# Layer 1 attention: where the gate product, the one-column scale steps and the near blocks' units are computed

## The chip, the cores and the metric

The kernel runs on one core of a Trainium2 chip. Its engines are TensorE (PE in the profile, with its weight loads as PEld), VectorE (DVE), ScalarE (ACT) and GpSimd (POOL); SyncE (SP) issues the DMAs. Each engine works through a list of its own in order and waits on semaphores for the others. The metric is the device time of one execution in microseconds, as the median of the runs.

## The reference

Two decoder layers and a final norm, on 1024 positions of width 1024 with 16 heads of 64. Layer 0 is attention with a forget gate; layer 1, to which this change belongs, is attention with three branches per head: over compressed blocks, over chosen blocks, and over a window of the last 512 positions. Its core, cut:

```python
lg = jnp.einsum('btgrd,btgnld->btgrnl', qc, kb).astype(jnp.float32) * scale   # chosen blocks
p = jax.nn.softmax(jnp.where(m, lg, NEG).reshape(...), axis=-1)
...
lg_w = jnp.einsum('bnqgrd,bnkgd->bngrqk', qb, k_band).astype(jnp.float32) * scale   # window
p_w = jax.nn.softmax(jnp.where(m_w[None, :, None, None], lg_w, NEG), axis=-1)
...
g = jax.nn.sigmoid(gate_raw).reshape(B, S, G, R, N_BRANCH)
o = g[..., 0:1] * o_c + g[..., 1:2] * o_s + g[..., 2:3] * o_w
return (o.reshape(B, S, W) * jax.nn.silu(z)) @ w_out
```

## The kernel before, in words

The program runs layer 0, then the projections and the compressed branch of layer 1, then the stage this change is about, and last the output projection with the final norm. In that stage `NsaSuper(h, s)` stands for one head `h` and one half `s` of the positions (512 queries), and the 32 of them run in order, `s` = 1 ahead of `s` = 0 in each head.

Each has eight units, `unit(y, qi)`: `qi` counts four tiles of 128 queries, `y` = 0 is the chosen blocks (128 to 1024 keys), `y` = 1 the window, here called the near blocks (128 to 640 keys). A unit goes from engine to engine. PE makes the scores `S` in PSUM (L1662). One custom DVE instruction (L1670) multiplies the scores by a scalar, adds a mask, writes the result to `P` in SBUF and keeps the minimum of each row; a second instruction of the same line reads that minimum out into `m`. For `y` = 0 the scalar of L1670 is a column of per-partition values (`units`), for `y` = 1 it is the constant 1.0, and the units come in afterwards: L1672 multiplies `m` by `units` and adds a constant. ACT then takes the exponential in place (L1673), with `m` as its bias and, for `y` = 1, a column of `units` as its scale, and sums each row into `l`. For `y` = 1 POOL splits the result into two halves of lower precision (L1676 the high part, L1677 the rest, into a ring of three `hl` buffers), and an SP transpose brings them to `hT`. For `y` = 0 PE transposes into `ptp` (L1695), ACT and DVE split that into `pth` and `ptl` (L286, L287). PE multiplies both with the values into `O` (L1703 to L1705).

`finish()` closes a group of eight units: DVE takes the reciprocals of the eight row sums per partition (L1735), multiplies them by the gates (L1736), and later multiplies `O` by the product (L1738, into `u`); POOL adds the two branches (L1739).

Between these units the list is filled with work of the layer's `z` projection (`nz`, L269 to L271). For each of its eight column blocks `nz_scale(p)` computes a scale on one column per partition in seven short DVE steps (L1475, two in `half_root` at L222 and L224, L1477 to L1481); `z_scale(p)` at L597 does likewise in layer 0. `zq`, in the profile `nzq`, is the small tile of these columns.

The order on each engine is set ahead of time: `run_attn` interleaves the units of the next group with the steps of this one, `merge` mixes in the filler by the costs that the generators yield, and a scheduler then places the instructions by its own account of when each could run.

Of the kernel before, what the change touches and what calls it, by code (L numbers as in the profile page):

```python
# [13 lines left out]
AF = mybir.ActivationFunctionType  # L14
OP = mybir.AluOpType
# [18 lines left out]
LNUP = 15 * 0.6931471805599453  # L34
# [7 lines left out]
def tile_fox_nsa(ctx, tc, a, out):  # L42
    nc = tc.nc
    V, A, G, T = nc.vector, nc.scalar, nc.gpsimd, nc.tensor
# [12 lines left out]
    def ps_s2(name):  # L57
        return psS.tile([P, 2, 512], F32, tag="S", name=name)
# [22 lines left out]
    ready = {}  # L81
# [6 lines left out]
    class Norm:  # L88
# [11 lines left out]
        def finish(self, g, parts=1, eng=None):  # L100
            st, h, x = self.st, self.h, self.x
            if self.n == 2:
                V.tensor_tensor(st[:, 0:1], st[:, 0:1], st[:, 1:2], OP.add)
            A.activation(st[:, 2:3], st[:, 0:1], AF.Sqrt, bias=eps, scale=1.0 / D)
            V.reciprocal(st[:, 3:4], st[:, 2:3])
            for i in range(parts):
                c = slice(i * D // parts, (i + 1) * D // parts)
                if eng is None:
                    V.scalar_tensor_tensor(h[:, c], x[:, c], st[:, 3:4], g[:, c], OP.mult, OP.mult)
                else:  # L110
                    eng.tensor_scalar(h[:, c], x[:, c], st[:, 3:4], 1.0, OP.mult, OP.mult)
                    eng.tensor_tensor(h[:, c], h[:, c], g[:, c], OP.mult)
            return h
# [105 lines left out]
    def half_root(q, c):  # L219


        V.tensor_scalar(q[:, c + 1:c + 2].bitcast(I32), q[:, c:c + 1].bitcast(I32), 24, 23,  # L222
                        OP.logical_shift_right, OP.logical_shift_left)
        V.tensor_scalar(q[:, c + 2:c + 3].bitcast(I32), q[:, c + 1:c + 2].bitcast(I32), 0x3F800000, None, OP.bitwise_xor)  # L224

    late_on = tc.keep_in_program_order
# [366 lines left out]
    def z_scale(p):  # L593


        zq = ready["zt", p]["q"]
        late_on(V.tensor_tensor(zq[:, 2:3], zq[:, 0:1], zq[:, 1:2], OP.add))  # L597
        half_root(zq, 2)
        V.tensor_scalar(zq[:, 5:6], zq[:, 4:5], 2.0 ** 46, None, OP.mult)
        V.scalar_tensor_tensor(ao[0][:, p:p + 1], zq[:, 3:4], 2.0 ** 81, ready["v", p][1], OP.mult, OP.mult)  # L600
        ready["c", p] = zq[:, 5:6]
# [387 lines left out]
    gates = pers.tile([P, NT, 48], F32, name="gates")  # L989
# [481 lines left out]
    def nz_scale(p):  # L1471


        zq = ready["zt", p]["q"]
        late_on(V.tensor_tensor(zq[:, 2:3], zq[:, 0:1], zq[:, 1:2], OP.add))  # L1475
        half_root(zq, 2)
        V.tensor_scalar(zq[:, 5:6], zq[:, 4:5], 2.0 ** 74, None, OP.mult)  # L1477
        V.tensor_tensor(zq[:, 6:7], zq[:, 5:6], ready["limits"][:, p // 2:p // 2 + 1], OP.mult)
        V.tensor_scalar(zq[:, 6:7], zq[:, 6:7], 2.0 ** 100, None, OP.min)
        V.tensor_scalar(zq[:, 7:8].bitcast(I32), zq[:, 6:7].bitcast(I32), 0x7F800000, None, OP.bitwise_xor)  # L1480
        V.tensor_scalar(ao1[:, p:p + 1], zq[:, 7:8], 0.5, None, OP.mult)  # L1481
        ready["c", p] = zq[:, 6:7]
# [120 lines left out]
    bias = []  # L1603
# [4 lines left out]
    class NsaSuper:  # L1608
# [30 lines left out]
        def unit(self, y, qi):  # L1639
            h, s, g = self.h, self.s, self.g  # L1640
            if self.first:
                self.pre()
                self.first = False
            k = KV[g, y][0]
            i = 4 * s + qi
            nm = f"{self.name}_{y}_{qi}"
            k0 = P * max(0, i - 4) if y else 0
            n = P * (i + 1) - k0
            ps = ps_s2(f"S_{nm}")
            if y:  # L1650
                L = at.tile([P, 640], F32, tag="Pw", bufs=5, name=f"P_{nm}")[:, 0:n]
            else:
                L = at.tile([P, n], F32, tag=f"P{s}{qi}", bufs=1, name=f"P_{nm}")
            m = at.tile([P, 1], F32, tag="m", bufs=8, name=f"m_{nm}")
            mk = bias[qi] if s and not y else wmask[:, 640 - n:]
            w = n if n <= 512 else n // 2
            if (h, s, y, qi) == (H - 1, 0, 1, 3):
                ready["scores"] = True
            c = 0
            for b in range(n // w):  # L1660
                for x in range(2):
                    T.matmul(ps[:, b, 0:w], self.q[x][:, qi * P:(qi + 1) * P], k[:, k0 + b * w:k0 + b * w + w],  # L1662
                             start=(x == 0), stop=(x == 1))
                c += 2 * max(107, w * 0.42)
            if w == n:
                src, dst, mk = ps[:, 0, 0:n], L, mk
            else:
                src, dst, mk = ps[:, :, 0:w], *(x.rearrange("p (a k) -> p a k", a=2) for x in (L, mk))
            unit, minus = ready["units"][0:2]
            V.tensor_tensor_reduce(dst, src, mk, 1.0 if y else unit, 3e38, OP.add, OP.min, m)  # L1670
            if y:
                V.tensor_scalar(m, m, unit, LNUP, OP.mult, OP.add)  # L1672
            A.activation(L, L, AF.Exp, bias=m, scale=minus if y else -1.0, accum_out=self.l[:, y, qi:qi + 1])  # L1673
            if y:
                hl = at.tile([P, 1280], F16, tag="hl", bufs=3, name=f"hl_{nm}")
                G.tensor_copy(hl[:, 0:n], L)  # L1676
                G.tensor_tensor(hl[:, n:2 * n], L, hl[:, 0:n], OP.subtract)  # L1677
                b = 2 * n // P
                nc.sync.dma_start_transpose(self.hT[:, self.at:self.at + b, :], hl[:, 0:2 * n])
                self.Ps[y, qi] = self.at, k0  # L1680
                self.at += b
            else:
                self.Ps[y, qi] = L, k0
            yield c
# [45 lines left out]
        def finish(self):  # L1730
            h, s, l = self.h, self.s, self.l
            p, j = h // 2, h % 2
            if j == 0:
                self.O[p, s, "t"] = at.tile([P, 4, P], F32, tag="ot", bufs=2, name=f"ot_{self.name}")
            V.reciprocal(l, l)  # L1735
            V.tensor_tensor(l, l, gates[:, 4 * s:4 * s + 4, 3 * h + 1:3 * h + 3].rearrange("p q y -> p y q"), OP.mult)  # L1736
            u = at.tile([P, 4, 2, 64], F32, tag="u", bufs=1, name=f"u_{self.name}")
            V.tensor_tensor(u, self.po, l.rearrange("p y q -> p q y")[:, :, :, None].to_broadcast([P, 4, 2, 64]), OP.mult)  # L1738
            G.tensor_tensor(self.O[p, s, "t"][:, :, 64 * j:64 * j + 64], u[:, :, 0], u[:, :, 1], OP.add)  # L1739
            if j and s == 0:  # L1740
                ready["done", p] = True
# [163 lines left out]
```

## Time and profile before

| | |
|---|---|
| median of 3 runs | 1460.36 us (1455.6 to 1462.95) |
| profiled execution | 1458.12 us, its span 1456.2 us |
| busy over the span | PE 94%, PEld 64%, DVE 77%, ACT 63%, POOL 40% |
| stage of the change | about 960 to 1385 us of the span |

A row of the grouped view names the line, engine, operation, tiles and shape, then the count; behind the bar stand the busy microseconds and the mean nanoseconds of one, then the idle time of that engine just before them and what ended it. The chain of waits is followed back from the last instruction: at each step to what released it, or to the instruction ahead of it on its engine. PE's busy time includes the tails of pipelined matmuls.

### The profile page before, as it was taken

Reading aid. Unit: us, or ns where it says so; the run is one execution under the profiler, and the core shown is the slowest. Engines: PE = TensorE matmul, PEld = TensorE weight load, DVE = VectorE, ACT = ScalarE, POOL = GpSimd, SP = SyncE. Lnnn points to the kernel's source line nnn. Section 1 sums busy time; section 2 is a strip of 40 time slices with the busy share of each in tenths; the row PEclk is TensorE's granted clock in tenths of the full one; section 3 lists DMA queues with packets and bytes.
Section 4 is the critical chain, followed back from the end, with each engine's and each line's share of the span. In section 5 each row is a group of like instructions: output and inputs, shape, how many; then the busy total and the mean of one; then the engine's idle time right before and its main releaser. Section 6 shows DMA issues by size and latency. Waiting matters only on the chain. (4 is left out here: it accounts for less than half of the span.)

```text
span 1456.2 us, 30393 instructions
## 1 busy us (share of the span) xinstructions
PE 1368.0 (94%) x10499; PEld 928.0 (64%) x10499; DVE 1120.3 (77%) x3016; ACT 915.9 (63%) x2328; POOL 585.3 (40%) x781
## 2 busy tenths in 40 slices
PE   5999999999999989999999988889999999998998
PEld 4778888888888745445545544446666766666643
DVE  6587787787878698486757677878999899989834
ACT  5376667776767665155555475667877778778512
POOL 2142433434334251231203456245766766765500
PEclk9999999999999999999999999999999999999999
DMA  5379798898988999354654446454667676776434
GB/s 197 96 164 191 188 185 199 203 186 198 189 197 180 244 230 203 107 176 151 189 174 141 134 121 159 119 148 92 135 151 164 140 171 123 135 169 150 95 109 145
DMA packets 414922, 234.72 MB, mean 161 GB/s; under 512 B 334448, under 2 KB 372656, under 8 KB 414768
## 3 DMA queue, kind: packets, MB, share of 16 engines
q1 hardware_dynamic: 414768, 232.78, 67.1%
q8 instruction: 83, 1.36, 0.4%
q14 instruction: 71, 0.58, 0.1%
HBM read 120.31 MB, written 28.38 MB: 102 GB/s over the span
## 5 line engine op out<-in xcount | busy, mean ns | idle before, releaser
L1662 PE MATMUL S_n<-nk,nq 128*128 128x320 f16 (+5 forms) x768 | 154.6, 314 | 13.5 <-DVE m_n L1670 12.6
L785 ACT ACTIVATE P<-P,m 128x512 f32<-128x512 f32 (+1 forms) x192 | 116.3, 607 | 53.9 <-DVE m L776 52.6
L1677 POOL TENSOR_TENSOR hl_n<-P_n,hl_n 128x640 f16<-128x640 f32 (+4 forms) x128 | 144.8, 1132 | 10.0
L756 POOL TENSOR_TENSOR Bd<-B,tri 128x128 f32<-128x128 f32 x128 | 62.4, 502 | 205.8 <-DVE m L776 189.3
L787 DVE SCALAR_TENSOR_TENSOR hl<-P,hl 128x512 f16<-128x512 f32 (+1 forms) x192 | 116.0, 620 | 28.7 <-ACT hl L786 27.2
L1676 POOL CAST hl_n<-P_n 128x640 f16<-128x640 f32 (+4 forms) x128 | 76.4, 597 | 122.1 <-ACT P_n L1673 97.3
L1673 ACT ACTIVATE P_n<-P_n,m_n 128x640 f32<-128x640 f32 (+7 forms) x128 | 98.7, 771 | 30.2 <-DVE m_n L1670 29.6
L1673 ACT ACTIVATE P_n<-P_n,m_n,units 128x640 f32<-128x640 f32 (+4 forms) x128 | 100.1, 782 | 22.5 <-DVE m_n L1672 20.6
L1662 PEld LDWEIGHTS <-nq 128*128 128x128 f16 x768 | 71.4, 98 | 60.4 <-issue 25.5
L286 ACT ACTIVATE pth_n<-ptp_n 128x512 f16<-128x512 f32 (+1 forms) x160 | 85.1, 545 | 38.9 <-PE ptp_n L1695 38.3
L287 DVE SCALAR_TENSOR_TENSOR ptl_n<-ptp_n,pth_n 128x512 f16<-128x512 f32 (+1 forms) x160 | 99.6, 632 | 7.9 <-ACT pth_n L286 5.9
L1695 PE MATMUL ptp_n<-ident,P_n 128*128 128x128 f32 x576 | 93.2, 279 | 7.5 <-ACT P_n L1673 2.2
L786 ACT ACTIVATE hl<-P 128x512 f16<-128x512 f32 (+1 forms) x192 | 92.4, 512 | 1.9 <-DMA pT<-hl 0.5
L1670 DVE CUSTOM_DVE_ANT_0 P_n<-S_n,wmask 128x640 f32<-128x640 f32 (+4 forms) x128 | 83.1, 650 | 7.2 <-PE S_n L1662 6.3
L1695 PEld LDWEIGHTS ptp_n<-ident,P_n 128*128 128x128 f32 x576 | 64.9, 141 | 33.4 <-DVE ptl_n L287 7.3
L183 ACT ACTIVATE sq<-sq,zg 128x512 f32<-128x512 f32 (+2 forms) x73 | 59.5, 815 | 22.8 <-DMA sq<-in_nsa_w_dram 17.8
L1703 PE MATMUL O_n<-nv,pth_n 128*128 128x64 f16 x576 | 71.7, 193 | 1.0 <-ACT pth_n L286 0.6
L97 ACT ACTIVATE h_n<-xr 128x512 f32<-128x512 f32 x32 | 20.0, 625 | 83.6 <-DVE xr L1795 41.4
L1704 PE MATMUL O_n<-nv,pth_n 128*128 128x64 f16 x576 | 71.8, 193 | 0.0
L1670 DVE CUSTOM_DVE_ANT_0 P_n<-S_n,bias,units 128x640 f32<-128x640 f32 (+1 forms) x64 | 68.8, 1074 | 2.9 <-PE S_n L1662 2.3
L1705 PE MATMUL O_n<-nv,ptl_n 128*128 128x64 f16 x576 | 68.7, 193 | 0.9 <-DVE ptl_n L287 0.9
L767 PE MATMUL S<-KH,Q 128*128 128x512 f32 (+1 forms) x192 | 65.0, 354 | 2.6 <-DVE m L776 2.3
(514 smaller groups left out, 4731.6 us busy)
## 6 DMA issues: line engine op xcount, KB each, us to landing
sq<-in_nsa_w_dram SPq DMA_DIRECT2D x40, 256.0 KB
B<-cD SPq DMA_DIRECT2D x16, 512.0 KB
nq<-qD SPq DMA_DIRECT2D x64, 128.0 KB
x<-in_x_dram SPq DMA_DIRECT2D x8, 512.0 KB
wst_k<-in_fox_w_dram SPq DMA_DIRECT2D x8, 512.0 KB
wst_v<-in_fox_w_dram SPq DMA_DIRECT2D x8, 512.0 KB
sq<-in_fox_w_out_dram SPq DMA_DIRECT2D x16, 256.0 KB
wst_q<-in_fox_w_dram SPq DMA_DIRECT2D x8, 512.0 KB
```

Source lines behind the costliest of these rows:

```text
L286: A.activation(hi[:, 0:n], pt[:, 0:n], AF.Copy, scale=scale)
L287: V.scalar_tensor_tensor(lo[:, 0:n], pt[:, 0:n], scale, h, OP.mult, OP.subtract)
L785: A.activation(L[:, 0:n], L[:, 0:n], AF.Exp, bias=init, scale=-1.0, accum_out=self.lr[:, col + c:col + c + 1])
L786: A.activation(hi[:, cs], L[:, 0:n], AF.Copy, scale=UP)
L787: V.scalar_tensor_tensor(lo[:, cs], L[:, 0:n], UP, hi[:, cs], OP.mult, OP.subtract)
L1662: T.matmul(ps[:, b, 0:w], self.q[x][:, qi * P:(qi + 1) * P], k[:, k0 + b * w:k0 + b * w + w], start=(x == 0), stop=(x == 1))
L1670: V.tensor_tensor_reduce(dst, src, mk, 1.0 if y else unit, 3e38, OP.add, OP.min, m)
L1673: A.activation(L, L, AF.Exp, bias=m, scale=minus if y else -1.0, accum_out=self.l[:, y, qi:qi + 1])
L1676: G.tensor_copy(hl[:, 0:n], L)
L1677: G.tensor_tensor(hl[:, n:2 * n], L, hl[:, 0:n], OP.subtract)
L1695: T.transpose(pt[:, (x + i) * P:(x + i + 1) * P], L[:, kb * P - k0:(kb + 1) * P - k0], ident)
L1704: T.matmul(o, hi, v[:, 64:128], start=False, stop=False)
```

## The change

Three things are written otherwise; the formula that is computed is that of before.

1. The product of reciprocals and gates (L1736) is issued on POOL instead of DVE.
2. In the steps on single columns, an addition of two columns (L597, L1475) becomes a form with one column as a per-partition scalar operand; in `nz_scale` the product with `limits` and the limit by a constant (L1478, L1479) become one such instruction.
3. For `y` = 1 the units become the scalar of L1670, as for `y` = 0. L1672 then only adds a constant, and ACT's exponential has the constant -1.0 as its scale.

```diff
@@ -594,7 +594,7 @@ z_scale
-        late_on(V.tensor_tensor(zq[:, 2:3], zq[:, 0:1], zq[:, 1:2], OP.add))
+        late_on(V.tensor_scalar(zq[:, 2:3], zq[:, 0:1], zq[:, 1:2], None, OP.add))
@@ -1472,11 +1472,10 @@ nz_scale
-        late_on(V.tensor_tensor(zq[:, 2:3], zq[:, 0:1], zq[:, 1:2], OP.add))
+        late_on(V.tensor_scalar(zq[:, 2:3], zq[:, 0:1], zq[:, 1:2], None, OP.add))
         half_root(zq, 2)
         V.tensor_scalar(zq[:, 5:6], zq[:, 4:5], 2.0 ** 74, None, OP.mult)
-        V.tensor_tensor(zq[:, 6:7], zq[:, 5:6], ready["limits"][:, p // 2:p // 2 + 1], OP.mult)
-        V.tensor_scalar(zq[:, 6:7], zq[:, 6:7], 2.0 ** 100, None, OP.min)
+        V.tensor_scalar(zq[:, 6:7], zq[:, 5:6], ready["limits"][:, p // 2:p // 2 + 1], 2.0 ** 100, OP.mult, OP.min)
@@ -1666,11 +1665,11 @@ NsaSuper.unit
-            unit, minus = ready["units"][0:2]
-            V.tensor_tensor_reduce(dst, src, mk, 1.0 if y else unit, 3e38, OP.add, OP.min, m)
+            unit = ready["units"][0]
+            V.tensor_tensor_reduce(dst, src, mk, unit, 3e38, OP.add, OP.min, m)
             if y:
-                V.tensor_scalar(m, m, unit, LNUP, OP.mult, OP.add)
-            A.activation(L, L, AF.Exp, bias=m, scale=minus if y else -1.0, accum_out=self.l[:, y, qi:qi + 1])
+                V.tensor_scalar(m, m, LNUP, None, OP.add)
+            A.activation(L, L, AF.Exp, bias=m, scale=-1.0, accum_out=self.l[:, y, qi:qi + 1])
@@ -1733,7 +1732,7 @@ NsaSuper.finish
-            V.tensor_tensor(l, l, gates[:, 4 * s:4 * s + 4, 3 * h + 1:3 * h + 3].rearrange("p q y -> p y q"), OP.mult)
+            G.tensor_tensor(l, l, gates[:, 4 * s:4 * s + 4, 3 * h + 1:3 * h + 3].rearrange("p q y -> p y q"), OP.mult)
```

The scheduler places the instructions anew. Behind the edit at L1478 the lines of the changed kernel have a number lower by one.

On POOL, at head 7, half 1, the product comes to stand between the two halves of the split of the group's last near block (`hl`, key tile 3). Before:

```order
L1627 TENSOR_SCALAR bias_11357<-selb 128x896
L1739 TENSOR_TENSOR ot_n_0_15180<-u_n_0_15183 128x4x64
L1676 CAST hl_n_1_1_3_15146<-P_n_1_1_3_15137 128x640
L1677 TENSOR_TENSOR hl_n_1_1_3_15146<-P_n_1_1_3_15137,hl_n_1_1_3_15146 128x640
L1676 CAST hl_n_0_1_0_15234<-P_n_0_1_0_15227 128x128
```

After:

```order
L1738 TENSOR_TENSOR ot_n_0_15176<-u_n_0_15179 128x4x64
L1675 CAST hl_n_1_1_3_15142<-P_n_1_1_3_15133 128x640
L1735 TENSOR_TENSOR l_n_1_14979<-l_n_1_14979,gates 128x8
L1676 TENSOR_TENSOR hl_n_1_1_3_15142<-P_n_1_1_3_15133,hl_n_1_1_3_15142 128x640
L1675 CAST hl_n_0_1_0_15230<-P_n_0_1_0_15223 128x128
```

One row is added, and the second half of the split now stands behind it.

On DVE, at the end of head 6, half 1, with the fourth column block's scale among it (`nzq`). Before:

```order
L1735 RECIPROCAL l_n_1_14448<-l_n_1_14448 128x8
L1672 TENSOR_SCALAR m_n_0_1_1_14753<-m_n_0_1_1_14753,units 128x1
L1475 TENSOR_TENSOR nzq_13610<-nzq_13610 128x1
L1736 TENSOR_TENSOR l_n_1_14448<-l_n_1_14448,gates 128x8
L222 TENSOR_SCALAR nzq_13610<-nzq_13610 128x1
L287 SCALAR_TENSOR_TENSOR ptl_n_1_0_14676<-ptp_n_1_0_14670,pth_n_1_0_14675 128x512
```

After:

```order
L1734 RECIPROCAL l_n_1_14445<-l_n_1_14445 128x8
L1671 TENSOR_SCALAR m_n_0_1_1_14750<-m_n_0_1_1_14750 128x1
L1475 TENSOR_SCALAR nzq_13608<-nzq_13608 128x1
L287 SCALAR_TENSOR_TENSOR ptl_n_1_0_14673<-ptp_n_1_0_14667,pth_n_1_0_14672 128x512
L287 SCALAR_TENSOR_TENSOR ptl_n_1_1_14682<-ptp_n_1_1_14676,pth_n_1_1_14681 128x512
L222 TENSOR_SCALAR nzq_13608<-nzq_13608 128x1
```

The product is gone from DVE, the addition has its new form, and the two `ptl` moved ahead of the next short step.

On PE, where head 7's first scores (`S`, half 1, chosen blocks, key tile 0) meet head 6's last products with the values (`O`). Before, two of the four score matmuls stand some 180 rows ahead of the other two:

```order
L270 MATMUL nz_1_14660<-hT_1_7605,zw_7998 128x512
L271 LDWEIGHTS zw_7998
L271 MATMUL nz_1_14660<-hT_1_7605,zw_7998 128x512
L1662 LDWEIGHTS nq_7_1_14978
L1662 MATMUL S_n_1_0_0_14985<-nk_0_13075,nq_7_1_14978 128x320
L1662 LDWEIGHTS nq_7_1_14979
```

After, all four stand together behind those products:

```order
L1704 MATMUL O_n_1_14706<-nv_1_13079,hT_n_1_14446 128x64
L270 LDWEIGHTS zw_7998
L270 MATMUL nz_1_14657<-hT_1_7605,zw_7998 128x512
L271 LDWEIGHTS zw_7998
L271 MATMUL nz_1_14657<-hT_1_7605,zw_7998 128x512
L1661 LDWEIGHTS nq_7_1_14974
L1661 MATMUL S_n_1_0_0_14981<-nk_0_13073,nq_7_1_14974 128x320
L1661 LDWEIGHTS nq_7_1_14975
L1661 MATMUL S_n_1_0_0_14981<-nk_0_13073,nq_7_1_14975 128x320
```

Heads 7, 9 and 11 had their first scores apart like this; now head 5 alone has.

## The prediction

> **What bounds the kernel now.** I first cut the span into the stage of the change and what lies around it, in the view by windows (span, then busy time of PE, PEld, DVE, ACT and POOL).
>
> ```profile
> 960.00:1385.00 425.00, 398.10 (x5011) 278.18 (x5010) 386.37 (x1053) 322.35 (x750) 266.72 (x315) 1.00 0.66 140
> 0.00:960.00 960.00, 905.64 (x5194) 620.96 (x5194) 704.87 (x1909) 578.45 (x1536) 317.45 (x465) 0.98 0.70 173
> ```
>
> In the stage DVE is busy 386.4 of 425 us (91%) and PE 398.1 (94%); ahead of it DVE has 73%. So a microsecond of DVE is worth most here, and nearly the whole change lies here. But PE has only 26.9 us free by this view. Two engines that full take turns, and the waits of the stage show it (who waited for whom: us, times, longest):
>
> ```profile
> ACT P_n L1673 <- DVE m_n L1670: 29.6, 47, 2.5
> ACT P_n L1673 <- DVE m_n L1672: 20.6, 30, 2.1
> PE S_n L1662 <- DVE m_n L1670: 12.6, 29, 1.0
> DVE P_n L1670 <- PE S_n L1662: 10.8, 26, 0.8
> DVE l_n L1735 <- ACT P_n L1673: 7.3, 13, 1.0
> PEld ptp_n L1695 <- DVE ptl_n L287: 7.3, 25, 0.9
> POOL hl_n L1676 <- ACT P_n L1673: 97.3, 53, 8.5
> ```
>
> ACT waits 50 us for DVE's minima, PE 12.6 for a score buffer that DVE holds; DVE in turn waits 10.8 for scores and 7.3 for exponentials. POOL is never the one that a long row waits for, and it stands idle 97 us ahead of the casts. Next I read the chain of waits in this stage (its shares by line, then single pieces: start, us, what):
>
> ```profile
> by line: PE S_n L1662 12.8%; DVE P_n L1670 11.6%; PE ptp_n L1695 10.1%; ACT P_n L1673 8.9%; issue 7.7%; DVE ptl_n L287 5.7%; PE O_n L1703 4.2%; PE O_n L1705 4.0%; PE O_n L1704 3.9%; PE nz L269 2.9%; PE nz L270 2.9%; PE nz L271 2.8%; ACT pth
> ...
> 991.89 0.63 DVE nzq L1475
> ...
> 999.35 0.71 DVE l_n L1736
> ...
> 1037.22 1.06 DVE l_n L1736
> ...
> 1050.69 0.83 DVE l_n L1736
> ...
> 1278.67 1.22 DVE nzq L1475
> ```
>
> ```profile
> 1350.67 0.29 DVE l_n L1736
> ```
>
> The chain changes between PE, DVE and ACT all the time: no engine alone bounds the stage. The gate product L1736 is on it in 19 pieces, from 999.35 to 1350.67, 7.1 us in all; the addition L1475 in all its 8, from 991.89 on, 4.8 us. That is a lot for products of 8 columns and sums of one. The order of time shows why (DVE, then POOL):
>
> ```profile
> 1050.69 0.83 DVE L1736 TENSOR_TENSOR l_n<-l_n,gates 128x8 f32<-128x8 f32 x1
> 1051.44 0.28 DVE L1670 CUSTOM_DVE_ANT_0 P_n<-S_n,wmask 128x128 f32<-128x128 f32 x1
> ```
>
> ```profile
> 1050.10 1.40 POOL L1677 TENSOR_TENSOR hl_n<-P_n,hl_n 128x640 f16<-128x640 f32 x1
> ```
>
> L1736 ends at 1051.52, as POOL's subtraction does (1051.50), and DVE's next minimum pass starts just then: a DVE instruction with two tensors in SBUF stands still for the rest of a POOL instruction.
>
> **The change part by part.** First what leaves DVE (by shape; busy us, mean ns):
>
> ```profile
> L1736 DVE TENSOR_TENSOR l_n<-l_n,gates 128x8 f32<-128x8 f32 x32 | 14.7, 458 | 0.7
> L1475 DVE TENSOR_TENSOR nzq<-nzq 128x1 f32<-128x1 f32 x8 | 5.4, 672 | 0.0
> L1478 DVE TENSOR_TENSOR nzq<-nzq,limits 128x1 f32<-128x1 f32 x8 | 2.6, 326 | 0.1
> L1672 DVE TENSOR_SCALAR m_n<-m_n,units 128x1 f32<-128x1 f32 x128 | 26.4, 206 | 1.3
> L1479 DVE TENSOR_SCALAR nzq<-nzq 128x1 f32<-128x1 f32 x8 | 1.1, 143 | 0.0
> ```
>
> The gate products: 32 x 458 ns = 14.7 us of DVE go, 7.1 of them on the chain. The scale steps: L1475, L1478 and L1479 take 5.4 + 2.6 + 1.1 = 9.1 us. Their two successors have a column as scalar operand, for which L1672 is the nearest row, 206 ns: 16 x 206 = 3.3, so 5.8 us of DVE go. On the chain L1475 falls from 4.8 to 8 x 0.206 = 1.6: 3.2 us.
>
> Does the new form escape POOL? The view of a line (least, median and largest ns) says so:
>
> ```profile
> L1672 DVE TENSOR_SCALAR m_n<-m_n,units x128: 192/205/215, 965.4 to 1373.4; 128x1 f32<-128x1 f32 x128
> ```
>
> ```profile
> L250 DVE TENSOR_SCALAR un<-ao,un x2: 232/717/1202, 517.5 to 1314.9; 128x8 f32<-128x8 f32 x2
> ```
>
> 128 instructions with POOL 63% busy (266.7 of 425) and none above 215 ns. With eight columns (L250) the same form took 232 once and 1202 once, so it is the single column that escapes. The Trainium skill (SBUF — State Buffer, Who interferes with whom) says that tensor_scalar too can enter a two-port mode, and that it then blocks against GpSimd like an instruction with two SBUF inputs; by that rule the new forms would stall as the old ones and the sum would lose its 3.2. For eight columns the trace agrees, for one it does not, so I take 206.
>
> The near blocks. The minimum pass gets a column as its scalar, L1672 loses it, and ACT's exponential loses one:
>
> ```profile
> L1670 DVE CUSTOM_DVE_ANT_0 P_n<-S_n,wmask,units 128x512 f32<-128x512 f32 x16 | 11.9, 741 | 0.0
> L1670 DVE CUSTOM_DVE_ANT_0 P_n<-S_n,wmask 128x512 f32<-128x512 f32 x16 | 11.0, 685 | 6.1 <-PE S_n L1662 5.6 <-POOL ot_n L1761 0.5
> ...
> L1670 DVE CUSTOM_DVE_ANT_0 P_n<-S_n,wmask,units 128x128 f32<-128x128 f32 x16 | 5.4, 338 | 0.0
> L1670 DVE CUSTOM_DVE_ANT_0 P_n<-S_n,wmask 128x128 f32<-128x128 f32 x16 | 4.5, 283 | 0.8 <-PE S_n L1662 0.5
> L1477 DVE TENSOR_SCALAR nzq<-nzq 128x1 f32<-128x1 f32 x8 | 1.2, 147 | 0.0
> L1673 ACT ACTIVATE P_n<-P_n,m_n,units 128x640 f32<-128x640 f32 x64 | 58.6, 916 | 12.3 <-DVE m_n L1672 12.0
> L1673 ACT ACTIVATE P_n<-P_n,m_n 128x640 f32<-128x640 f32 x16 | 13.3, 830 | 7.8 <-DVE m_n L1670 7.5
> ```
>
> With a column the pass takes 741 against 685 ns at 512 keys, 338 against 283 at 128: 55 to 56 ns more, 128 x 0.056 = +7.2 us. L1672 with constants alone is like L1477, 147 ns: 128 x (0.206 - 0.147) = -7.6. On DVE the two cancel, and the minimum is ready as early as before. ACT gains 916 - 830 = 86 ns each, 128 x 0.086 = 11.0 us. ACT has 103 us idle here, so only those on the chain count. L1673 is 8.9% of it, 37.8 us; all its exponentials come to 98.7 + 100.1 us on the page's two rows of L1673:
>
> ```profile
> L1673 ACT ACTIVATE P_n<-P_n,m_n 128x640 f32<-128x640 f32 (+7 forms) x128 | 98.7, 771 | 30.2 <-DVE m_n L1670 29.6
> L1673 ACT ACTIVATE P_n<-P_n,m_n,units 128x640 f32<-128x640 f32 (+4 forms) x128 | 100.1, 782 | 22.5 <-DVE m_n L1672 20.6
> ```
>
> So about 37.8 / 198.8 = 19% are on the chain, and 19% of 11.0 is 2.1 us.
>
> What POOL gets: 32 products of 8 columns. No row of POOL is that small. Nearest are the subtractions L1677:
>
> ```profile
> L1677 POOL TENSOR_TENSOR hl_n<-P_n,hl_n 128x640 f16<-128x640 f32 x64 | 92.6, 1446 | 4.8
> L1677 POOL TENSOR_TENSOR hl_n<-P_n,hl_n 128x128 f16<-128x128 f32 x16 | 6.8, 428 | 1.3
> ```
>
> A line through both (1.99 ns a column) leaves 0.19 us at 8 columns; the smallest row itself, 0.43, is the upper end. I take 0.2, the row's own slope: 6.4 us in all (13.8 at most), inside the 97.3 us that POOL idles ahead of casts. Without that cover they would delay each group's last subtraction, its transpose and the window products. `u` is in no hurry for the product (DVE):
>
> ```profile
> 1062.69 0.20 DVE L1735 RECIPROCAL l_n<-l_n 128x8 f32<-128x8 f32 x1 [1.03 <-ACT P_n L1673]
> ```
>
> ```profile
> 1075.88 0.68 DVE L1738 TENSOR_TENSOR u_n<-O_n,l_n 128x512 f32<-128x512 f32 x1
> ```
>
> The multiplication that answers to this reciprocal starts 13 us later. On POOL the product waits for the reciprocal, and behind it stands one subtraction (front part, POOL's order); the reciprocal takes 0.2 us and the cast ahead runs beside it.
>
> In layer 0 eight additions get the new form: 8 x 0.06 us by the same two rows (206 against 147), 0.5 us at most, on a DVE that is 73% busy: nothing. The moved rows on PE I price by two heads fewer whose first scores lie apart, two score matmuls and two `nz` products each, below 1 us a head: between -2 and +2, taken as nothing.
>
> **The sum.** On the chain: 7.1 + 3.2 + 2.1 = 12.4 us. That would be the gain if no other path stood close behind, but one does: PE has 26.9 us free in 425, and the reciprocal just ahead of the product had found DVE idle 13 times of 32, waiting for ACT, so DVE is not always the late one there. What is late next is PE's score and transpose matmuls, and the minimum pass that waits for them. Ends: nothing, or all DVE time that goes, 14.7 + 5.8 + 0.4 = 20.9 us. I take the chain's figure less a quarter, 9 us. The profiled execution took 1458.1 us (span 1456.2 and 1.9 around it), so its like would take 1449.1; the median shown is 2.2 above that execution, 1451.3 by it. I forecast 1450.
>
> **The rivals.** (a) DVE bounds the stage throughout: each microsecond freed is one gained. For it: the 50 us of ACT's waits for DVE, and the pieces of L1736 on the chain. Against it: DVE waits for scores 26 times. 1460.4 - 20.9 = 1439.5.
>
> (b) PE takes over: freed DVE time becomes DVE idle time ahead of L1670 and L287. For it: PE at 94%; against it: PE waits for DVE's buffers 29 times and for `ptl` 25 times, 20 us. The gain would be a third of the chain's, 4 us: 1456.
>
> (c) The column form stalls as the two-tensor form did, the rule cited above. The gain loses its 3.2 us on the chain: 1451.3 + 3.2 = 1454.5. Against it: the 128 even durations of L1672.
>
> (d) Slower: POOL becomes a link. The product waits on POOL for a reciprocal that stands in DVE's list behind other work; the subtraction behind it, its transpose and the window products come late, and PE waits at L1703. It decides once the delay eats the slack between reciprocal and `u`. With 32 groups and, as an estimate, 0.7 us each (half a subtraction of 1.4 us): 22 us, less the 9: 1473. Against it: POOL's 97 us and the 13 us above.
>
> **How the numbers follow.** My forecast, a gain of 7.5 to 14 us, has 0.40, with a range of its own of 1446 to 1453; (a) 0.15, (b) 0.25, (c) 0.08, (d) 0.10; 0.02 is left for a plain miss on the slow side. A measurement of this kernel can tell about 0.5%, 7.3 us: faster means below 1453.1. Faster: 0.40 + 0.15 = 0.55; same: 0.25 + 0.08 = 0.33; slower: 0.12. The range takes in (a) at its low end and (b) and (c) with 5 us for moved rows and spread at the other: 1439 to 1461.
>
> **What would show it.** In the changed profile: L1736 absent from DVE and 32 POOL products near 0.2 us; L1475 and the joined step even at about 0.2; passes with `units` at 640 keys near 0.87 us and the correction near 0.15; exponentials of 640 keys at 830 ns; DVE's busy time in the stage lower by about 20 us, and the stage shorter by 9. If DVE's busy time falls and the stage does not, (b) holds, and the waits of L1670 for scores will have grown. If `u` or L1703 waits for POOL or for transposes, (d). If the moved rows of PE cost more than their price, the forecast is wrong without any of these.

## The result and the profile after

| kernel | median us (lowest to highest) | ratio to the kernel before, 95% interval |
|---|---|---|
| before | 1459.2 (1451.45 to 1463.69) | 1 |
| changed | 1451.45 (1446.08 to 1456.11) | 0.9949 [0.9935, 0.9963] |
| changed, once more, beside 1459.47 | 1448.09 (1446.82 to 1454.64) | 0.9932 [0.9917, 0.9948] |

The change takes 0.51% (7.4 us) off the time in the first comparison and 0.68% (9.9 us) in the second. The forecast was 1450 with a gain of 9; of the gains that it gave as its own, 7.5 to 14 us, the first comparison just misses the lower end.

First what each piece became. The groups by shape in the stage of the changed kernel (behind the bar: busy us, mean ns of one; then the idle time before it):

```profile
L1672 ACT ACTIVATE P_n<-P_n,m_n 128x640 f32<-128x640 f32 x80 | 66.0, 825 | 14.2 <-DVE m_n L1671 11.0 <-DVE m_n L1669 2.9
...
L1669 DVE CUSTOM_DVE_ANT_0 P_n<-S_n,wmask,units 128x640 f32<-128x640 f32 x64 | 56.1, 877 | 0.2 <-PE S_n L1661 0.2
...
L1671 DVE TENSOR_SCALAR m_n<-m_n 128x1 f32<-128x1 f32 x128 | 18.8, 147 | 1.1
...
L1735 POOL TENSOR_TENSOR l_n<-l_n,gates 128x8 f32<-128x8 f32 x32 | 7.0, 219 | 0.3 <-DVE m_n L1671 0.3
...
L1478 DVE TENSOR_SCALAR nzq<-nzq,limits 128x1 f32<-128x1 f32 x8 | 1.7, 207 | 0.1
L1475 DVE TENSOR_SCALAR nzq<-nzq 128x1 f32<-128x1 f32 x8 | 1.6, 204 | 0.0
```

The single steps are at 204 and 207 ns, where their two-tensor forms took 672 and 326. The gate product takes POOL 219 ns in place of 458 on DVE. The minimum pass of 640 keys is at 877, the correction at 147, the exponential at 825.

Then the stage. Its ends are the first and the last multiplication `u`, which every group of a head ends with. The line's view, of the kernel before and of the changed one (least, median and largest ns; then first and last start):

```profile
L1738 DVE TENSOR_TENSOR u_n<-O_n,l_n x32: 634/680/692, 985.8 to 1381.4; 128x512 f32<-128x512 f32 x32
```

```profile
L1737 DVE TENSOR_TENSOR u_n<-O_n,l_n x32: 651/691/694, 988.6 to 1375.1; 128x512 f32<-128x512 f32 x32
```

From 395.6 us it came down to 386.5, by 9.1. The first `u` came 2.8 us later in this execution, so the span shrank by 6.2 only (1456.2 to 1450.0). In the second comparison's profile the stage is 386.4 long and begins at 984.9.

Third, the engines in the middle of the stage, in the view by windows (span, busy time of PE, PEld, DVE, ACT, POOL), before and changed:

```profile
1000.00:1300.00 300.00, 287.80 (x3690) 204.11 (x3690) 273.60 (x748) 232.61 (x547) 197.68 (x237) 1.00 0.68 143
```

```profile
1000.00:1300.00 300.00, 293.39 (x3766) 210.71 (x3765) 266.86 (x739) 233.04 (x567) 206.38 (x269) 1.00 0.72 148
```

In the same 300 us PE does 76 instructions more (2.1%) and is busy for 293.4 us (98%) instead of 287.8; DVE falls from 273.6 to 266.9. The waits of the changed stage say the same (who waited for whom: us, times, longest):

```profile
DVE P_n L1669 <- PE S_n L1661: 15.5, 38, 1.2
DVE l_n L1734 <- ACT P_n L1672: 8.5, 14, 0.9
...
PE S_n L1661 <- DVE m_n L1669: 8.1, 14, 1.9
...
DVE u_n L1737 <- PE O_n L1704: 5.4, 10, 1.2
...
PE O_n L1702 <- DMA hT_n<-hl_n: 1.5, 1, 1.5
...
DVE u_n L1737 <- POOL l_n L1735: 0.5, 1, 0.5
```

PE's waits for a score buffer fell from 12.6 us (29 times) to 8.1 (14 times). DVE's waits for scores rose from 10.8 (26 times) to 15.5 (38 times), and `u`, which had waited 1.6 us for the products on PE, now waits 5.4. The profile of the second comparison repeats these numbers (15.1, 37 times; 8.1, 14 times; 5.4), so they belong to the kernel and not to one execution. `u` waited for POOL once, 0.5 us.

That PE took over the stage does not follow from this. The chain of waits, by engine and as a share of the whole span, before and changed (it goes back to about 770 us in both):

```profile
PE 22%; DVE 14%; ACT 6%; issue 3%; POOL 1%; DMA 1%; SPq 0%; DVEq 0%; ACTq 0%; POOLq 0%
```

```profile
PE 20%; DVE 15%; ACT 5%; issue 3%; DMA 2%; POOL 1%; SPq 0%; DVEq 0%; ACTq 0%; POOLq 0%
```

Summed from the first `u` to the last, PE's pieces went from 189.3 us of 395.6 to 172.0 of 386.5. What came onto the chain is DMA transposes and POOL: together 3.3 us before, 18.8 in the changed kernel and 31.9 in the second comparison's profile.

### The profile page after: what moved, and what is told of

Same layout as the page of the kernel before. It is cut to its first block, busy times and chain, and to the rows that moved or that the text cites. A ratio compares the mean times of both kernels' runs of the same rounds, so it can differ in the third digit from the quotient of the medians.

```text
span 1450.0 us, 30377 instructions
## 1 busy us (share of the span) xinstructions
PE 1360.2 (94%) x10499; PEld 928.2 (64%) x10499; DVE 1105.2 (76%) x2976; ACT 906.4 (63%) x2328; POOL 590.8 (41%) x813
## 5 line engine op out<-in xcount | busy, mean ns | idle before, releaser
L1672 ACT ACTIVATE P_n<-P_n,m_n 128x640 f32<-128x640 f32 (+7 forms) x256 | 186.9, 731 | 50.1 <-DVE m_n L1669 26.9
L1669 DVE CUSTOM_DVE_ANT_0 P_n<-S_n,wmask,units 128x640 f32<-128x640 f32 (+2 forms) x192 | 124.4, 656 | 12.4 <-PE S_n L1661 11.2
L768 PE MATMUL S<-KL,Q 128*128 128x512 f32 (+1 forms) x192 | 64.7, 349 | 0.0
```

What stands on the lines that cost most here:

```text
L1669: V.tensor_tensor_reduce(dst, src, mk, unit, 3e38, OP.add, OP.min, m)
L1672: A.activation(L, L, AF.Exp, bias=m, scale=-1.0, accum_out=self.l[:, y, qi:qi + 1])
```

## The experiments

Three theories stood at the start. **A**: the pieces of the chain of waits pay, all at the rate of the whole change in the first comparison. **B**: what counts is DVE's busy time, about half of which is paid out, so the near blocks' edit, which leaves DVE's time nearly as it was, brings nothing. **C**: the gain is luck of the new order, and the parts alone bring anything. The first three runs make one part of the change each.

**The gate product alone.**

```diff
-            V.tensor_tensor(l, l, gates[:, 4 * s:4 * s + 4, 3 * h + 1:3 * h + 3].rearrange("p q y -> p y q"), OP.mult)
+            G.tensor_tensor(l, l, gates[:, 4 * s:4 * s + 4, 3 * h + 1:3 * h + 3].rearrange("p q y -> p y q"), OP.mult)
```

> The kernel before with the gate product alone on POOL. Theory A (what counts is the stall's pieces on the chain of waits, paid out at the rate of the whole change, 7.75 us of 12.4): 7.1 x 0.63 = 4.4 us faster, 1455. Theory B (DVE's own time counts, at the stage's rate of about one half): 14.7 / 2 = 7 us faster, 1452. Theory C (the gain comes from the scheduler's new order, not from the stalls): no relation to either, and the three parts alone do not add up to 7.75.

**The one-column steps alone** (the addition in `z_scale` is edited in the same way).

```diff
-        late_on(V.tensor_tensor(zq[:, 2:3], zq[:, 0:1], zq[:, 1:2], OP.add))
+        late_on(V.tensor_scalar(zq[:, 2:3], zq[:, 0:1], zq[:, 1:2], None, OP.add))
...
-        V.tensor_tensor(zq[:, 6:7], zq[:, 5:6], ready["limits"][:, p // 2:p // 2 + 1], OP.mult)
-        V.tensor_scalar(zq[:, 6:7], zq[:, 6:7], 2.0 ** 100, None, OP.min)
+        V.tensor_scalar(zq[:, 6:7], zq[:, 5:6], ready["limits"][:, p // 2:p // 2 + 1], 2.0 ** 100, OP.mult, OP.min)
```

> The kernel before with the one-column steps alone changed. Theory A: 3.2 x 0.63 = 2.0 us faster, 1457. Theory B: 5.8 / 2 = 2.9 us faster. Theory C: anything within 5 us either way.

**The units in the minimum pass alone.**

```diff
-            unit, minus = ready["units"][0:2]
-            V.tensor_tensor_reduce(dst, src, mk, 1.0 if y else unit, 3e38, OP.add, OP.min, m)
+            unit = ready["units"][0]
+            V.tensor_tensor_reduce(dst, src, mk, unit, 3e38, OP.add, OP.min, m)
             if y:
-                V.tensor_scalar(m, m, unit, LNUP, OP.mult, OP.add)
-            A.activation(L, L, AF.Exp, bias=m, scale=minus if y else -1.0, accum_out=self.l[:, y, qi:qi + 1])
+                V.tensor_scalar(m, m, LNUP, None, OP.add)
+            A.activation(L, L, AF.Exp, bias=m, scale=-1.0, accum_out=self.l[:, y, qi:qi + 1])
```

> The kernel before with the near blocks' units alone inside the minimum pass. Theory A: 2.1 x 0.63 = 1.3 us faster, 1458. Theory B: DVE's time is unchanged, so nothing, 1459. Theory C: anything within 5 us either way.

| part alone, beside 1458.63 | median us | ratio, 95% interval | gain by the ratio | piece of the chain | A | B |
|---|---|---|---|---|---|---|
| gate product | 1452.95 | 0.9961 [0.9947, 0.9976] | 5.7 | 7.1 | 4.4 | 7 |
| one-column steps | 1455.8 | 0.9976 [0.9965, 0.9988] | 3.5 | 3.2 | 2.0 | 2.9 |
| units | 1456.83 | 0.9978 [0.9964, 0.9992] | 3.2 | 2.1 | 1.3 | 0 |

All three intervals lie below 1. Each reaches some 2 us to either side, so the gate product and the steps fit A and B alike; only the units' interval (1.2 to 5.2 us) leaves out B's figure. The line of `u` in the three profiles, gate product, steps and units in turn:

```profile
L1738 DVE TENSOR_TENSOR u_n<-O_n,l_n x32: 650/688/692, 983.8 to 1375.8; 128x512 f32<-128x512 f32 x32
```

```profile
L1737 DVE TENSOR_TENSOR u_n<-O_n,l_n x32: 634/680/692, 987.5 to 1379.2; 128x512 f32<-128x512 f32 x32
```

```profile
L1738 DVE TENSOR_TENSOR u_n<-O_n,l_n x32: 677/683/693, 990.6 to 1383.3; 128x512 f32<-128x512 f32 x32
```

The stage lasts 392.0, 391.7 and 392.7 us against 395.6: 3.6, 3.9 and 2.9 less, 10.4 in all; the three edits together took 9.1. By the times the parts add up to 12.4 us, and the whole brought 7.4 and 9.9. So most of the parts' gain survives their sum. A bit is lost in all three comparisons, but with some 2 us for each part the sum of 12.4 is uncertain by 3 to 4, and beside the 9.9 the loss is not clear of that.

Is the units' 3.2 us the exponentials' doing, as A has it? The groups by shape of that kernel hold a second candidate, in instructions that it did not touch:

```profile
L1736 DVE TENSOR_TENSOR l_n<-l_n,gates 128x8 f32<-128x8 f32 x32 | 10.8, 338 | 0.7
...
L1475 DVE TENSOR_TENSOR nzq<-nzq 128x1 f32<-128x1 f32 x8 | 4.7, 591 | 0.0
L1478 DVE TENSOR_TENSOR nzq<-nzq,limits 128x1 f32<-128x1 f32 x8 | 2.0, 252 | 0.1
```

The gate products, still on DVE there, take 10.8 us instead of 14.7, and the two steps 1.3 less: in the new order they met POOL less often. So 5.2 us of DVE stalls went by placement, beside ACT's 11.0 us (915.9 to 904.9 on the pages). On this kernel's chain of waits the gate product has 10 pieces with 2.9 us, where it had 19 with 7.1. The run does not tell which of the two paid. The same holds in small for the steps' kernel, whose gate products fell to 13.2. What is saved on gate products here cannot be saved again where they leave DVE; that alone can make the parts add up to more than the whole, without any help of PE. B, which gave the units nothing, is not refuted by this gain, and C is right in so far as the order decides how long these instructions stall. That each part brings something, and the gate product most, stands.

**A column as scalar, or two tensors.** Is it the form of the instruction that escapes POOL? Two kernels add the same one-column sum to the changed one, behind the reciprocal in all 32 groups; nothing uses it. The first has two SBUF tensors, the second a column as scalar:

```diff
             V.reciprocal(l, l)
+            x = at.tile([P, 1], F32, tag="x1", bufs=3, name=f"x_{self.name}")
+            V.tensor_tensor(x, l[:, 0, 0:1], l[:, 0, 1:2], OP.add)       # first
+            V.tensor_scalar(x, l[:, 0, 0:1], l[:, 0, 1:2], None, OP.add) # second
```

> The changed kernel with 32 extra DVE sums of one column, a form with two tensors in SBUF, each behind a reciprocal of row sums; their results go nowhere. Stall theory: each stands still for the rest of a POOL instruction as the gate product did, some 400 to 500 ns, and the gate product's part of the gain is given back: 4 to 6 us slower than the change, 1455 to 1457. If an extra instruction costs its own 150 ns and no more: 1 to 2 us slower, as the next kernel.

> The same 32 extra sums in the form with one column as scalar operand. Stall theory: 206 ns each whatever POOL does, 1 to 2 us slower than the change, 1452 to 1454, and 3 to 4 us faster than the kernel with two tensors. If the count of DVE instructions is what matters and not the form: the same time as that kernel.

The two lines in their profiles:

```profile
L1736 DVE TENSOR_TENSOR x_n<-l_n x32: 148/416/981, 982.0 to 1372.7; 128x1 f32<-128x1 f32 x32
```

```profile
L1736 DVE TENSOR_SCALAR x_n<-l_n x32: 203/213/216, 980.9 to 1367.6; 128x1 f32<-128x1 f32 x32
```

The two-tensor sum takes anything from 148 ns to 981, 366 in the mean (400 to 500 were expected); the other never leaves 203 to 216. The order of time shows what ends the long ones. The longest sum of the first kernel, and what runs on POOL beside it:

```profile
1049.85 0.98 DVE L1736 TENSOR_TENSOR x_n<-l_n 128x1 f32<-128x1 f32 x1
```

```profile
1049.42 1.40 POOL L1676 TENSOR_TENSOR hl_n<-P_n,hl_n 128x640 f16<-128x640 f32 x1
```

POOL's subtraction ends at 1050.82 and the sum at 1050.83. A sum of the second kernel beside the same subtraction, in the same group:

```profile
1048.40 0.21 DVE L1736 TENSOR_SCALAR x_n<-l_n 128x1 f32<-128x1 f32 x1
```

```profile
1047.96 1.40 POOL L1676 TENSOR_TENSOR hl_n<-P_n,hl_n 128x640 f16<-128x640 f32 x1
```

This sum is done 0.75 us before POOL. Counted over all 32: in the first kernel 27 sums start while a POOL instruction runs, and 25 of these end 5 to 27 ns behind it; in the second 29 start so, and 28 of these end ahead of it. So the even durations are the form's, not the place's, and the long ones are waits for POOL. In time the two are 1454.91 (0.9978 [0.9966, 0.9991]) and 1451.89 (0.9960 [0.9947, 0.9972]) beside 1457.55: 3.0 us apart by the medians, 2.6 by the ratios, for 32 x 0.16 = 5.0 us of DVE. The intervals touch, so the size is rough. Beside the change's first ratio they are 4.2 and 1.6 us slower, within the 4 to 6 and 1 to 2 expected; beside the second, 6.7 and 4.1.

**POOL later.** If POOL were a link, more work in front of the product would cost time. This kernel adds an unused sum of 256 columns to POOL in each group:

```diff
             V.reciprocal(l, l)
+            x = at.tile([P, 256], F32, tag="x1", bufs=1, name=f"x_{self.name}")
+            G.tensor_tensor(x, l[:, 0, 0:1].to_broadcast([P, 256]), l[:, 0, 1:2].to_broadcast([P, 256]), OP.add)
             G.tensor_tensor(l, l, gates[:, 4 * s:4 * s + 4, 3 * h + 1:3 * h + 3].rearrange("p q y -> p y q"), OP.mult)
```

> The changed kernel with an extra POOL sum of 256 columns, some 0.7 us, ahead of each gate product; its result goes nowhere. It waits for the reciprocal as the product does and holds up the near blocks' last subtraction and the product. If POOL's idle time covers it: within 2 us of the change, 1450 to 1454. If POOL has become a link (rival d): 32 x 0.7 = 22 us slower, or at least 10.

```profile
L1736 POOL TENSOR_TENSOR x_n<-l_n x32: 607/611/1058, 976.3 to 1369.5; 128x256 f32<-128x256 f32 x32
```

It took 1451.03 us, 0.9954 [0.9941, 0.9968] beside 1457.55. The 32 sums of 0.61 us lengthened POOL's busy time by 17.6 us (590.8 to 608.4) and the time by 0.7 us beside the change's first ratio and 3.2 beside the second, far from the 10 to 22 of a POOL that is a link. The order of time in the changed kernel shows the room (start, us, engine):

```profile
1148.74 0.20 DVE L1734 RECIPROCAL l_n<-l_n 128x8 f32<-128x8 f32 x1 [0.23 <-ACT P_n L1672]
...
1160.30 0.65 DVE L1737 TENSOR_TENSOR u_n<-O_n,l_n 128x512 f32<-128x512 f32 x1
```

```profile
1151.88 0.20 POOL L1735 TENSOR_TENSOR l_n<-l_n,gates 128x8 f32<-128x8 f32 x1
```

The product runs 3 us behind its reciprocal, and `u` needs it 8 us later.

**Less work for PE, with and without the change.** Where did the rest of the gain go? If to PE, then work taken from PE must pay more behind the change than ahead of it. The near blocks' third product with the values (the low half of the split) is left out, 480 products, in the changed kernel and in the one before:

```diff
-        def pv(self, qi, y, kb, hi, lo, last=False):
+        def pv(self, qi, y, kb, hi, lo, last=False, low=True):
...
-            T.matmul(o, hi, v[:, 64:128], start=False, stop=False)
-            T.matmul(o, lo, v[:, 0:64], start=False, stop=last)
+            T.matmul(o, hi, v[:, 64:128], start=False, stop=last and not low)
+            if low:
+                T.matmul(o, lo, v[:, 0:64], start=False, stop=last)
...
-                self.pv(qi, 1, k0 // P + k, self.hT[:, b + k, :], self.hT[:, b + n + k, :], qi == 3 and k == n - 1)
+                self.pv(qi, 1, k0 // P + k, self.hT[:, b + k, :], self.hT[:, b + n + k, :], qi == 3 and k == n - 1, False)
```

> The changed kernel without the third product of the near blocks' values (the low half of the split times the high half of the values): 480 matmuls of 64 columns, which follow each other every 0.03 us, 14 us of PE less; the low half is still made and moved, and the output is less exact. If PE bounds the stage now: 8 to 14 us faster than the change, 1437 to 1443. If DVE still does: at most 4 us faster, 1447 or more.

> The kernel before, likewise without the near blocks' third product: 14 us of PE less, the output less exact. On the changed kernel the same cut brought 10.6 us. If the change moved the bound from DVE's stalls to PE: clearly less here, 4 to 8 us faster than before, 1450 to 1454. If PE bounded the stage as much before: the same 10 to 11 us, 1447.

In the changed kernel it gave 1439.5 us, 0.9876 [0.9863, 0.9889] beside 1457.55: against the change's two ratios 10.6 and 8.2 us. In the kernel before it gave 1454.51, 0.9965 [0.9952, 0.9978] beside 1459.47: 5.1 us. The line of `u`, on the changed kernel and on the one before:

```profile
L1738 DVE TENSOR_TENSOR u_n<-O_n,l_n x32: 641/684/692, 984.5 to 1362.3; 128x512 f32<-128x512 f32 x32
```

```profile
L1739 DVE TENSOR_TENSOR u_n<-O_n,l_n x32: 641/679/692, 984.9 to 1376.1; 128x512 f32<-128x512 f32 x32
```

The stage is 8.7 us shorter than the changed one (377.8 against 386.5), and only 4.4 shorter than the one before (391.2 against 395.6). By the windows PE falls back to 289.4 of 300 us in the one and to 283.1 in the other. So by the totals a cut on PE pays about twice as much behind the change. The totals mislead, though. The 23rd `u` in the kernel before and its version with less work for PE, then in the changed kernel and its version:

```profile
1262.99 0.68 DVE L1738 TENSOR_TENSOR u_n<-O_n,l_n 128x512 f32<-128x512 f32 x1
```

```profile
1254.89 0.68 DVE L1739 TENSOR_TENSOR u_n<-O_n,l_n 128x512 f32<-128x512 f32 x1
```

```profile
1256.49 0.65 DVE L1737 TENSOR_TENSOR u_n<-O_n,l_n 128x512 f32<-128x512 f32 x1
```

```profile
1247.27 0.68 DVE L1738 TENSOR_TENSOR u_n<-O_n,l_n 128x512 f32<-128x512 f32 x1
```

Counted from the first `u`, the cut had brought 7.2 us by then ahead of the change (277.2 to 270.0) and 5.1 behind it (267.9 to 262.8). Between this `u` and the next one, 6.4 of the 7.2 us went again, in one place (order of time, then the view by windows, whose third number from the end is the granted clock of TensorE):

```profile
1265.43 0.23 PE L1703 MATMUL O_n<-nv,hT_n 128*128 128x64 f16 x1 [3.84 <-DMA hT_n<-hl_n]
```

```profile
1263.00:1272.00 9.00, 6.57 (x32) 3.87 (x33) 3.21 (x9) 2.69 (x6) 2.60 (x2) 0.62 0.78 139
```

PE stood still 3.84 us for a DMA transpose, and the granted clock was 0.62 there, after 1.00 from the first `u` to the 23rd. In its stage this kernel's PE waits 7.3 us for transposes in three places, the kernel before not at all. Its gate products also stall less, 11.7 us against 14.7. So in this execution a wait for a transpose and a lower clock halved the gain, and the pair does not show that PE took over. It shows that less work for PE pays with the change and without it.

**Less work for DVE behind the change.** The counterpart: the 128 corrections L1671 are left out.

```diff
-            if y:
-                V.tensor_scalar(m, m, LNUP, None, OP.add)
```

> The changed kernel without the addition of the constant to the near blocks' minima (line 1671): the near blocks' exponentials are then not scaled by 2 to the 15, numerator and sum alike, and only the rounding of the low half of the split differs. 128 DVE steps of 147 ns fewer, each on the way from the minimum to the exponential. If PE has taken over as the bound (rival b): at most 3 us faster than the change, 1449 to 1452. If DVE and the way through it still bound: 128 x 0.147 = 18.8 us of DVE, half of it paid out, 1442.

It took 1455.97 us (1449.9 to 1458.33), 0.9970 [0.9956, 0.9984] beside 1458.63, so 0.2 to 0.4% more than the change. Neither expectation holds: not at most 3 us faster, and not 1442. A part goes with the clock: its 12 runs had a granted clock of 0.984 in the mean, those of the change and of the kernel before 0.986. Among the runs of one kernel the time rises by about 0.9 us for each 0.001 less of the clock (an estimate, over all kernels here), which makes some 2 us; which of the two is the cause, the runs do not tell. Windows and waits of this kernel:

```profile
1000.00:1300.00 300.00, 289.58 (x3754) 209.11 (x3752) 261.98 (x637) 229.36 (x561) 202.16 (x265) 1.00 0.71 147
```

```profile
DVE P_n L1669 <- PE S_n L1661: 17.1, 38, 1.1
PE S_n L1661 <- DVE m_n L1669: 13.3, 20, 2.2
```

In these 300 us DVE is busy 4.9 us less than in the changed kernel, and PE is busy less too. PE waits longer for score buffers (13.3 us against 8.1) and DVE longer for scores. The line view of one product of two SBUF tensors, with `no`, in the changed kernel and in this one, shows what else became of DVE:

```profile
L1753 DVE SCALAR_TENSOR_TENSOR no<-no,nzq,nz x16: 740/748/1848, 1020.5 to 1378.9; 128x512 f32<-128x512 f32 x16
```

```profile
L1751 DVE SCALAR_TENSOR_TENSOR no<-no,nzq,nz x16: 748/1218/1942, 1019.1 to 1380.1; 128x512 f32<-128x512 f32 x16
```

Its median went from 748 to 1218 ns. The order of time shows one of them on DVE, and POOL beside it:

```profile
1019.12 1.94 DVE L1751 SCALAR_TENSOR_TENSOR no<-no,nzq,nz 128x512 f32<-128x512 f32 x1
1020.98 0.87 DVE L1669 CUSTOM_DVE_ANT_0 P_n<-S_n,wmask,units 128x640 f32<-128x640 f32 x1
```

```profile
1019.11 1.40 POOL L1674 TENSOR_TENSOR hl_n<-P_n,hl_n 128x640 f16<-128x640 f32 x1
```

Both start at 1019.1; POOL's subtraction lasts to 1020.51, and DVE ends 0.55 us later, which is about what is left of a product of 0.74. In the groups the 16 products come to 20.7 us instead of 13.3, and they hold 3.6% of this stage's chain (the score pass behind the one above waits for it). So 7.4 us came back in stalls that the new order brought. Nor were the 18.8 us all to be won: the records of neighbours on DVE overlap (above, the product ends at 1021.06 and the score pass starts at 1020.98), and in the changed kernel only 6.0 us of the corrections' 18.8 lie outside every other DVE record. On the pages DVE's busy time fell by 4.8 us (1105.2 to 1100.4). Why these bought nothing stays open; the order was not held.

**A version that relieves PE.** On the view that PE binds, the chosen blocks of half 0 were sent the near blocks' way: split on POOL, transposed by DMA, 160 instructions fewer on PE. The core of the edit:

```diff
-            self.blocks = pack([(0, kb, max(0, kb - 4 * s), 4) for kb in range(4 * s + 4)])
+            self.blocks = pack([(0, kb, max(0, kb - 4 * s), 4) for kb in range(4 * s + 4)]) if s else []
...
-            if y:
+            if y or not s:
                 hl = at.tile([P, 1280], F16, tag="hl", bufs=3, name=f"hl_{nm}")
```

> A version that follows from PE being the bound and POOL having 150 us idle in the stage: the changed kernel with the chosen blocks of the lower half (s = 0) taken the way of the near blocks, split by POOL and transposed by DMA, where before PE transposed them and ACT and DVE split the result. 160 of 576 PE transposes go (0.109 us apart, 17 us), with 48 ACT and 48 DVE instructions of the split; POOL gets 16 x 5 us, some 80 us, on 271 of 417; the s = 0 gates lose their factor. If PE bounds and POOL and the DMAs keep up: 8 to 15 us faster than the change, 1436 to 1443. If POOL or the transposes become a link: no faster than the change, 1451 or more.

> The changed kernel itself beside these two, so that the kernel without the constant (1456) can be told from a difference of chips. If that kernel's loss is its own: 1449 to 1453 here again. If the chips differ: 1454 to 1457.

It took 1521.56 us, 1.0430 [1.0413, 1.0447]; so the expectation for a link, 1451 or more, holds. The changed kernel beside it, the last row of the first table, came out a little under the 1449 to 1453 expected; that speaks against a difference of chips behind the 1455.97 above. The chain of waits of its stage, by line, and the waits:

```profile
by line: DMA hT_n<-hl_n 26.9%; POOL hl_n L1676 14.3%; POOL hl_n L1675 9.7%; issue 8.9%; DVE P_n L1669 7.2%; PE S_n L1661 5.6%; POOL ot_n L1740 2.9%; ACT P_n L1672 2.8%; PE ptp_n L1694 2.7%; DVE wo_nsa_w_out L714 1.9%; PE ptn_n L1753 1.8%; P
```

```profile
POOL hl_n L1675 <- DMA hT_n<-hl_n: 70.4, 52, 4.5
POOL hl_n L1675 <- ACT P_n L1672: 33.0, 21, 8.3
```

POOL's split and the DMA transposes hold half of the chain. POOL's casts wait 70.4 us for transposes to give a buffer back, 22.4 in the changed kernel. Whether more than three `hl` buffers would have helped was not tried. The granted clock was 0.93 from 960 to 1445 us, where the changed stage had 1.00, so a part of the loss may be the clock's. A milder version sends one of four query tiles of half 0 that way, and takes 64 instructions from PE (the core of the edit):

```diff
-            self.blocks = pack([(0, kb, max(0, kb - 4 * s), 4) for kb in range(4 * s + 4)])
+            self.blocks = pack([(0, kb, max(0, kb - 4 * s), 3 + s) for kb in range(5 * s + 3)])
...
-            if y:
+            if y or s == 0 and qi == 3:
                 hl = at.tile([P, 1280], F16, tag="hl", bufs=3, name=f"hl_{nm}")
```

> The same idea at two fifths of the size: the changed kernel with only the last tile of the lower half's chosen blocks (512 keys) split by POOL and transposed by DMA. 64 PE transposes go (7 us), POOL gets 16 x 1.8 = 28 us, the DMAs 16 more transposes of 128x1024. The larger version was 4% slower, with DMA transposes 30% of the chain of waits. If that was a ring of POOL and DMA that only fills at the larger size: 3 to 6 us faster than the change. If each unit that is sent this way puts the transposes on the path: slower than the change in proportion, 1465 to 1480.

```profile
by line: PE S_n L1661 11.3%; DVE P_n L1669 10.7%; PE ptp_n L1694 7.8%; ACT P_n L1672 7.2%; issue 7.1%; DMA hT_n<-hl_n 6.2%; POOL hl_n L1676 5.5%; DVE ptl_n L287 3.8%; ACT pth_n L286 3.2%; POOL hl_n L1675 3.2%; PE nz L269 3.1%; PE nz L270 2.
```

1458.77 us, 1.0008 [0.9991, 1.0025]: against the change's ratios 0.6 to 0.8% lost, neither the 3 to 6 us of gain nor the 1465 to 1480 that were expected. Transposes and splits are 15% of its chain. Of the kernels that compute the whole formula, none is faster than the change.

## Why the prediction was right, step by step

**The chain as the measure of the gain** was right in sum: pieces of 7.1, 3.2 and 2.1 us, 12.4 in all, and parts of 5.7, 3.5 and 3.2 when made alone. For the gate product and the steps this is the piece itself, within about 2 us; half of the DVE time that goes, 7 and 2.9 us, would have fitted these two as well, so the chain is borne out but not singled out. For the units it is not shown, since fewer stalls elsewhere could have paid as well.

**The discount of a quarter for PE** was right in size: 9 us forecast; 7.4 and 9.9 measured, 9.1 by the stage. Its reason, PE's score matmuls late next, is borne out by the waits alone: DVE waits longer for scores, but PE's part of the chain did not grow, and the two runs with less work for PE do not show it. DMA transposes and POOL came onto the chain, which the prediction had only as a sign of (d). The quarter was chosen and not worked out from a row, so that it came out is in part luck. The runs do not tell how much of the shortfall is PE's, how much the transposes', and how much comes from stalls that two parts both saved.

**The form of the one-column steps**: 206 ns taken, 204 and 207 measured; the pair of added sums shows that the form does it. Rival (c) is out. The Trainium skill (SBUF — State Buffer, Who interferes with whom) says that tensor_scalar can enter a two-port mode, and so contend with GpSimd, when its operands meet certain conditions; the prediction left the conditions out. Here a single column did not stall, with 203 to 216 ns in 32 executions.

**The near blocks**: 147 ns for the correction was exact, the exponentials came to 825 for 830, the passes of 640 keys to 877 where 870 was said.

**POOL**: 0.2 us a product was taken, 0.219 measured. `u` is in no hurry, as said, and 18 us more of POOL cost 0.7 to 3.2 us. Rival (d) is out at its price of 22 us a kernel. Its signs did show in small: `u` waited 0.5 us for POOL, PE 1.5 us for a transpose, and transposes came onto the chain.

**DVE's busy time**: 20.9 us were to go. The durations of the instructions that the change touches add up to 19.7 us less, but the pages fell by 15.1 (1120.3 to 1105.2), and the window from 960 to 1385 us by 12.2 (386.4 to 374.2) where about 20 had been said. Durations of other DVE instructions grew by 3.4, and the records overlap. The largest growth is the weights' L714, from 12.7 to 14.1 us; the rest is spread in tenths. The step left out that the untouched two-tensor instructions meet POOL anew in a new order. The forecast did not rest on this term; rival (a) did.

**Rival (a)**, DVE bounding throughout, gave 1439.5. It is out by the time, and by the score passes' longer waits for PE. **Rival (b)**, PE taking over, is out by its price of 4 us: the least gain that the first comparison's interval allows is 5.4 us, the second's 7.6. Its mechanism shows in DVE's longer waits for scores, and no run here shows more of it.

**The moved rows on PE** were priced at nothing, between -2 and +2 us. PE's side of it cannot be told from nothing. That was the wrong place to look for what a new order costs: it shows on DVE, where it took 5.2 us of stalls away in the units' kernel and added 7.4 on one line in the kernel without corrections.

## What to carry to other kernels

Where no engine bounds alone, the pieces of an edit on the chain of waits gave its gain here to within a few microseconds; then ask which engine's waits will grow, and take a part off. When a cut on one engine pays less in one kernel than in another, follow both in time before the totals are read: here a single wait for a transpose made the difference. When a scheduler lays a program anew, compare the mean durations of the instructions that were not edited as well: two-tensor DVE instructions beside POOL can hide a gain, or make one up, of the size that is looked for. Before work is sent to an engine that idles a lot, look at the DMA queue behind it: here POOL had idle time, and its casts waited for the transposes.

## What was not expected of the hardware

- A sum of one column with two SBUF tensors took 148 to 981 ns on DVE, in 32 executions of one line, while the same sum with one column as scalar took 203 to 216. At its best the two-tensor form is the faster one.
- A new order moved the stalls of untouched instructions by 5 to 7 us from kernel to kernel, nearly as much as the whole change brings. It repeats: the changed kernel's second profile has L714 at 14.1 us again.
- The DMA transposes came onto the chain as soon as the rest went faster. In the changed stage three pieces of the chain of waits stand there (start, us), none before; in the second comparison's profile there are five, and in the kernel before with less work for PE three.

```profile
1163.64 3.54 DMA hT_n<-hl_n
...
1261.01 3.77 DMA hT_n<-hl_n
...
1274.61 3.42 DMA hT_n<-hl_n
```

  PE waited for them 1.5 us in one place, and its weight loads 1.9 us in two, but the kernel that sent half 0's chosen blocks there as well took 4.3% more than the kernel before.
